# A scheduler's clock that counts stores with the loads, and a last weight matrix whose preparation yields between its steps

## The chip, the cores and the metric

The kernel runs on one core of one Trainium2 chip. The metric is the device time of one execution in microseconds. One execution was recorded by the hardware profiler; all durations below are from that record unless another source is named.

## The reference, cut to what matters

One layer of an encoder reads 2048 prompt frames and 64 frames of running streams. After a differential attention (branch A, result `oa`) and a retention (branch B, result `ob`), both of width 512, the layer ends like this:

```python
oa = (rmsnorm(oa, subln_g) * (1.0 - lam_init)).reshape(B, T, W_A) * jax.nn.silu(za)
ob = rmsnorm(ob).reshape(B, T, W_B) * jax.nn.silu(zb)
m = ga * (oa @ w_oa) + gb * (ob @ w_ob)     # w_oa, w_ob: 512 x 1024; ga, gb: sigmoid gates
return x + m @ w_out                        # w_out: 1024 x 1024
```

The two products with `w_oa` and `w_ob` are called the branch products here, and `w_out` is the last matrix. Everything is fp32.

## The kernel before, in words

**How order comes about.** The program is written by a planner that runs while the kernel is built. Work is cut into Python generators (tasks). `loop` takes the task with the lowest priority number that is not asleep, lets it emit its next instructions, and puts it to sleep until the time, or the condition, that it yields. The planner's clock is `self.pe`; it advances with each matmul emitted. Estimated ends on the other engines are kept in `self.act`, `self.dve`, `self.pool`, and the end of the loads in `self.dma`: `ld` adds a load's bytes at 230 or 300 bytes per ns to `self.dma`, and a load counts as landed `DMA_LAT` later. `st` gives a store its own time and leaves `self.dma` alone. A task that waits for a tile in memory sleeps until that estimate. What is emitted this way becomes a fixed order on PE, ACT, DVE and POOL, and each of them executes in that order, so an instruction whose data is late holds up all behind it. All DMAs are issued by one queue, SP.

**The high and low split.** Each fp32 operand of a matmul is split in two: ACT casts the high half (names in `h`), DVE or POOL subtracts it to get the low half (names in `l`). Each product takes three matmuls: high by high, high by low, low by high.

**The stage of the branch products** runs from about 1575 us to 1773 us. The columns are taken in 8 groups of 264 (256 prompt columns and 8 of the sample). For every group, `og_fin` brings in 4 tiles each of branch A and of branch B: DMA loads `z` and `on`, ACT takes the SiLU of `z`, POOL multiplies (`on`), ACT casts `ogh`, DVE subtracts `ogl`. Then `m_tile` computes 8 tiles of 128 output rows; a tile is 24 matmuls (lines 1722 to 1724), 12 into a bank with tag `mm` (branch A) and 12 into one with tag `s` (branch B); both tags have two banks. `m_fin` ends a tile: DVE multiplies each bank with its gate (`gt`, line 1742) and so frees the bank, POOL adds the two (line 1746), SP stores the sum into `mT` in HBM. The gates of a tile are loaded (`gaT`, `gbT`) and put through a tanh on ACT (line 1698). There are five pairs of gate tiles, so a pair is loaded again only when its store has landed. There is room for three half groups of `ogh`, `ogl` (tags `og` and `ob`): the half for branch B of the next group can be cast only when branch A of the last tile of the present group has been multiplied.

**The last matrix beside it.** `b_prep` works through `w_out` in four steps (c = 0 to 3). `b_raw` loads four 128x512 blocks (`wst`), of which DVE forms the sums and differences t1 to t4 of a seven-product scheme (line 1758), and `b_split` makes high and low halves: `bh`, `bl` of the plain blocks, `bht`, `blt` of the sums of c = 0, 1 (lines 1815, 1818), and, after the weights of the branch products are free, `wot` for those of c = 2, 3 (`b_late`). `b_prep` has priority 2, the branch products 8. In `out_prep`, which loads `z` and `on`, the condition `b_left < 13` lets the four loads of c = 0 go ahead of the second group.

**The last stage** (`y_group`, from about 1773 us) takes the groups again. `y_load` reads four blocks `a` of `mT` back per group, `y_prep` forms s1 and s2 on DVE and s3 and s4 on POOL (`a<-a`) and splits all of them (`ah` on ACT, `al` on DVE, line 1860); seven products P1 to P7 of 12 matmuls each follow (line 1934), in the order P1, P2, P6, P5, P7, P3, P4. `y_out` moves them: ACT copies `u`, POOL adds the loaded input `oxt` (line 1756), DVE adds the bank (line 1984: `u<-s` for P2, `u<-mm` for P7, `u<-at` for P3, `oxt<-mm` for P4). P4 of a group is followed on PE by P1 of the next.

Of the kernel before, what the change touches and what calls it, by code (L numbers as in the profile page):

```python
# [37 lines left out]
SLACK = 400.0  # L38
PACE = 700.0
DMA_LAT = 2600.0  # L40
QUANT = 6


# [16 lines left out]
class Hybrid:  # L60
# [72 lines left out]

    def ld(self, dst, src, nbytes=0):
        self.nc.sync.dma_start(dst, src)
        self.dma = max(self.dma, self.pe) + nbytes / (300.0 if self.opened else 230.0)
        return self.dma + DMA_LAT

    def st(self, dst, src, nbytes=0):
        self.nc.sync.dma_start(dst, src)  # L140
        return self.pe + nbytes / 150.0 + DMA_LAT

    def psum(self, tag):
        return self.pp.tile([128, 512], F32, tag=tag, name=tag, bufs=BUFS[tag])
# [1487 lines left out]
            yield self.pe  # L1632

    def out_prep(self):
        pa = self.z3p
        self.wo = [[([[self.sb(self.zq, [128, 512], "wa", "woq", F32R) for n in "hl"],
                      [pa.tile([128, 512], F32R, tag=f"wo{n}{br}{kt}", name=f"wo{n}{br}{kt}") for n in "hl"]], {})
                    for kt in range(4)] for br in range(2)]
        for br in range(2):
            yield from self.load_wo(br, 0)  # L1640
        for g in range(8):
            gsl = slice(GW * g, GW * g + GW)
            for br, (oT, zT) in enumerate(((self.oaT, self.zaT), (self.obT, self.zbT))):
                for kt in range(4):
                    yield from self.take("oz", 2)
                    on = self.sb(pa, [128, GW], "oz", "on")
                    z = self.sb(pa, [128, GW], "oz", "z")
                    self.ld(z, zT[kt][:, gsl], 1 << 17)
                    t = self.ld(on, oT[kt][:, gsl], 1 << 17)
                    og = []  # L1650
                    self.ogs.append(og)
                    self.spawn(self.og_fin(on, z, t, og, (2 * g + br) % 3 == 2), 1)
                    yield self.pe
            if g == 0:
                self.spawn(self.gates(), 0)
# [105 lines left out]
    def b_raw(self, c, pool, tag):  # L1761
        w = self.i["w_out"][0]
        raw = {}
        for k, r, n in (("11", c, 0), ("12", c, 512), ("22", c + 4, 512), ("21", c + 4, 0)):
            yield from self.take(tag)
            raw[k] = self.sb(pool, [128, 512], tag, "wst")
            t = self.ld(raw[k], w[128 * r:128 * r + 128, n:n + 512], 1 << 18)
            self.b_left -= 1
        yield t + 600
        return raw  # L1770

    def b_prep(self):
        late = []
        for c in range(4):
            raw = yield from self.b_raw(c, self.z4, "st")
            for k in ("t1", "t2"):
                yield from self.take("st")
                raw[k] = self.sb(self.z4, [128, 512], "st", "wst")
            t1 = self.add(False, ALU.subtract, raw["t1"], raw["12"], raw["11"], self.pe)
            for k in ("11", "21", "22"):  # L1780
                t = yield from self.b_split(k, c, raw[k], self.pe)
            t3 = self.add(False, ALU.subtract, raw["12"], raw["22"], raw["12"], t)
# [4 lines left out]
            yield t2  # L1787
            t4 = self.add(False, ALU.subtract, raw["21"], raw["21"], raw["t2"], t2)
            parts = [("t2", c, raw["t2"], t4), ("t1", c, raw["t1"], t1), ("t3", c, raw["12"], t3),
                     ("t4", c, raw["21"], t4)]  # L1790
            if c < 2:
                yield from self.b_fin(parts)
            else:
                late.append(parts)
        self.spawn(self.b_late([p for pair in zip(*late) for p in pair]), 1)
        self.spawn(self.y_prep(), 1)

    def b_fin(self, parts):
        for k, c, s, t in parts:
            t = yield from self.b_split(k, c, s, t)  # L1800
            self.give("st", t)

    def b_late(self, parts):
        yield lambda: self.q_end is not None
        yield self.q_end
        yield from self.b_fin(parts)
# [368 lines left out]
    def run(self):  # L2175
# [20 lines left out]
        self.b_left = 16  # L2196
        for k in ("ac", "u", "xt", "ob"):
            self.res[k].free = []
        self.q_end = self.smx = None
        self.y_at, self.yr = -1, []  # L2200
        self.yq = [{} for _ in range(8)]
        ET = mybir.EngineType
# [93 lines left out]
```

## Time and profile before

| what | value |
|---|---|
| median of 3 runs (lowest, highest) | 1945.87 us (1943.82, 1946.53) |
| the profiled execution: its own time, its span | 1945.82 us, 1944.0 us |
| PE busy, share of the span | 1927.5 us, 99% |
| DVE, ACT, POOL busy | 1166.6, 964.9, 490.1 us |
| moved by DMA, mean rate | 303.32 MB, 156 GB/s |
| granted TensorE clock, mean | 0.998 |

PE is busy nearly all the time, so time is lost where PE stands and where its clock is lowered; the other engines and the DMAs matter only where PE waits for them. "PE busy" takes in the modelled ends of the matmuls, which overlap. In a list of waits, the first name is who waits, the second for whom; the columns are the total in us, how often, and the longest. A row of a timeline gives the start, the duration, the engine, the line and the operation, `out<-in`, the count, and in brackets how long the engine had stood idle before and what ended that.

### The profile page before, as it was taken

To read this page: it belongs to the slowest core of one execution; us is meant where nothing else is said; L and a number is where in the kernel's file an instruction comes from. 1 tells how busy PE (TensorE), PEld (TensorE's weight loads), DVE (VectorE), ACT (ScalarE), POOL (GpSimd) and SP (SyncE) were. 2 spreads that over 40 slices of the span, in tenths; PEclk is the share of its full clock that TensorE was granted. 3 is DMA by queue.
4 is the path that set the end of the run, shared out by engine and by line. 5 is a ranking of instruction groups with operands and counts; after the bars stand their busy time and mean duration, and the time that the engine had idled before them with its cause. 6 is when DMAs were issued, how large, how long until landed. Compare 5 with 4: busy or idle time off the path is not lost.

```text
span 1944.0 us, 33842 instructions
## 1 busy us (share of the span) xinstructions
PE 1927.5 (99%) x11984; PEld 1731.2 (89%) x11984; DVE 1166.6 (60%) x2798; ACT 964.9 (50%) x2072; POOL 490.1 (25%) x429
## 2 busy tenths in 40 slices
PE   9999999999999999999999999999999999999999
PEld 8779999999988899999998888888888889998887
DVE  6753777646666336648856757845773376545643
ACT  7443766544434235535765646544563445653321
POOL 4310112112122121211121111112113356543422
PEclk9999999999999999999999999999999999999999
DMA  7747454335566655654344253363133678866651
GB/s 235 240 151 199 143 143 132 106 102 156 163 192 187 166 148 168 202 183 141 112 120 128 76 146 96 99 185 116 63 99 108 190 229 259 264 196 189 190 151 65
DMA packets 372074, 303.32 MB, mean 156 GB/s; under 512 B 77440, under 2 KB 334720, under 8 KB 371904
## 3 DMA queue, kind: packets, MB, share of 16 engines
q1 hardware_dynamic: 371904, 301.16, 52.6%
q8 instruction: 94, 1.54, 0.4%
q14 instruction: 76, 0.62, 0.1%
HBM read 195.87 MB, written 100.14 MB: 152 GB/s over the span
## 4 chain that ended last, share of the span: by engine, by line
PE 88%; DVE 5%; DMA 3%; POOL 1%; issue 1%; ACT 1%; SPq 1%; DVEq 0%; POOLq 0%; ACTq 0%
PE mm L554 51%; PE mm L1934 4%; PE s L1052 3%; PE s L1053 3%; PE at L1160 3%; PE at L1934 2%; PE pv L1139 2%; PE pv L1140 2%; PE pv L1138 2%; PE s L1934 1%; PE s L1723 1%; PE s L1724 1%; PE pv L1521 1%; PE mm L1723 1%; PE s L1722 1%
## 5 line engine op out<-in xcount | busy, mean ns | idle before, releaser
L514 POOL TENSOR_TENSOR wl<-ws,wh 128x512 fp32r<-128x512 f32 x191 | 261.4, 1380 | 896.2 <-ACT wh L504 544.9
L554 PE MATMUL mm<-xh,wh 128*128 128x512 f32 (+2 forms) x1280 | 460.7, 360 | 0.0
L554 PE MATMUL mm<-xh,wl 128*128 128x512 f32 (+2 forms) x1280 | 452.7, 354 | 0.0
L554 PE MATMUL mm<-xl,wh 128*128 128x512 f32 (+2 forms) x1280 | 451.9, 353 | 0.0
L554 PEld LDWEIGHTS mm<-xh,wl 128*128 128x128 f32 x1280 | 241.0, 188 | 31.7
L554 PEld LDWEIGHTS mm<-xh,wh 128*128 128x128 f32 x1280 | 241.4, 189 | 29.1 <-issue 0.2
L554 PEld LDWEIGHTS mm<-xl,wh 128*128 128x128 f32 x1280 | 241.6, 189 | 27.8
L554 PE MATMUL mm<-wh,xh 128*128 128x256 f32 (+1 forms) x768 | 236.7, 308 | 0.0
L554 PE MATMUL mm<-wh,xl 128*128 128x256 f32 (+1 forms) x768 | 231.3, 301 | 0.0
L554 PE MATMUL mm<-wl,xh 128*128 128x256 f32 (+1 forms) x768 | 231.0, 301 | 0.0
L1175 DVE TENSOR_TENSOR atl<-at,ath 128x512 fp32r<-128x512 f32 (+1 forms) x144 | 93.7, 659 | 136.2 <-ACT ath L1173 136.1
L504 ACT CAST wh<-ws 128x512 fp32r<-128x512 f32 x192 | 117.0, 617 | 112.6 <-PE mm L554 90.3
L1091 ACT ACTIVATE row<-row,a_mx 128x1024 f32<-128x1024 f32 (+7 forms) x160 | 153.7, 962 | 24.5 <-DVE a_mx L1071 24.3
L554 PEld LDWEIGHTS mm<-wh,xh 128*128 128x128 f32 x768 | 146.3, 190 | 7.1 <-issue 0.5
L554 PEld LDWEIGHTS mm<-wl,xh 128*128 128x128 f32 x768 | 146.4, 191 | 6.7 <-issue 0.5
L554 PEld LDWEIGHTS mm<-wh,xl 128*128 128x128 f32 x768 | 146.3, 190 | 5.5
L865 DVE TENSOR_TENSOR ev<-mm,rsb 128x512 f32<-128x512 f32 x140 | 83.0, 593 | 112.8 <-PE mm L554 112.4
L1173 ACT CAST ath<-at 128x512 fp32r<-128x512 f32 (+1 forms) x144 | 78.7, 563 | 141.5 <-PE at L1160 138.4
L1061 DVE CUSTOM_DVE_ANT_0 row<-s,dfar 128x512 f32<-128x512 f32 (+2 forms) x192 | 118.2, 630 | 46.4 <-PE s L1053 45.9
L1052 PE MATMUL s<-K,q 128*128 128x512 f32 (+3 forms) x320 | 118.4, 374 | 0.7 <-DVE a_acc L1061 0.7
L1053 PE MATMUL s<-K,q 128*128 128x512 f32 (+3 forms) x320 | 115.2, 362 | 0.0
L1110 ACT ACTIVATE row<-row,a_w 128x1024 f32<-128x1024 f32 (+4 forms) x96 | 85.1, 898 | 34.4 <-DVE a_w L1105 31.2
(342 smaller groups left out, 4193.5 us busy)
## 6 DMA issues: line engine op xcount, KB each, us to landing
ws<-in_w_in_dram SPq DMA_DIRECT2D x192, 256.0 KB, 3.1
q<-qT SPq DMA_DIRECT2D x128, 128.0 KB, 3.0
V<-vN SPq DMA_DIRECT2D x24, 512.0 KB, 5.4
K<-kT SPq DMA_DIRECT2D x48, 256.0 KB, 4.3
a<-mT SPq DMA_DIRECT2D x34, 256.0 KB, 4.1
gt<-gaT SPq DMA_DIRECT2D x64, 132.0 KB, 3.2
gt<-gbT SPq DMA_DIRECT2D x64, 132.0 KB, 3.1
mT<-gt SPq DMA_DIRECT2D x64, 132.0 KB, 3.0
```

What stands on the lines that cost most here:

```text
L504: self.nc.scalar.copy(h, st)
L514: self.nc.gpsimd.tensor_sub(l, st, h.bitcast(F32))
L554: nc.tensor.matmul(ps, p, q, start=c == 0 and i == 0, stop=c == KC - 1 and i == 2)
L865: nc.vector.tensor_mul(ev, ps, rsb)
L1052: nc.tensor.matmul(ps, q1s, kk, start=True, stop=False)
L1053: nc.tensor.matmul(ps, q2s, kk, start=False, stop=True)
L1061: nc.vector.tensor_tensor_reduce(out=units[k0 // 1024][:, k0 % 1024:k0 % 1024 + n], in0=ps, in1=tab, scale=-SLOPES[h], scalar=3.0e38, op0= ...
L1091: nc.scalar.activation(u, u, AF.Exp, bias=mx, scale=-1.0, accum_out=lp[:, k:k + 1])
L1110: nc.scalar.activation(u1, u1, AF.Identity, scale=w[:, 1:2])
L1173: nc.scalar.copy(ah[:, :w], at[:, :w])
L1175: nc.vector.tensor_sub(al[:, :w], at[:, :w], ah[:, :w].bitcast(F32))
L1934: nc.tensor.matmul(q[b], u, v, start=fresh and c == 0 and m == 0, stop=c == 3 and m == 2, skip_group_check=True)
```

## The change

Three things are changed, all in the planner; no arithmetic is added or taken away. From `out_prep` on (`packed`), loads count at 265 bytes per ns, and stores are counted on the same clock. The preparation of the last matrix yields for 1500 ns of the planner's clock between its loads and between its steps, and the condition `b_left` goes. `y_load`, which read `mT` back when all four `t4` were emitted, waits for three `t1`.

```diff
+RATE = 265.0
     def ld(self, dst, src, nbytes=0):
-        self.dma = max(self.dma, self.pe) + nbytes / (300.0 if self.opened else 230.0)
+        self.dma = max(self.dma, self.pe) + nbytes / (RATE if self.packed else 300.0 if self.opened else 230.0)
     def st(self, dst, src, nbytes=0):
-        return self.pe + nbytes / 150.0 + DMA_LAT
+        if self.packed:
+            self.dma = max(self.dma, self.pe) + nbytes / RATE
+        return max(self.packed * self.dma, self.pe + nbytes / 150.0) + DMA_LAT
     def out_prep(self):
+        self.packed = 1
...
-                yield lambda: self.b_left < 13
...     # b_raw, after each load
-            self.b_left -= 1
-        yield t + 600
+            yield self.pe + 1500
+        if t + 600 > self.pe:
+            yield t + 600
...     # b_prep, after t1, after each split, after t3 and t2; b_fin likewise for c < 2
+            yield self.pe + 1500
-            yield t3
+            yield max(t3, self.pe + 1500)
     def y_load(self):
-        yield lambda: len(self.wt["t4"]) == 4
+        yield lambda: len(self.wt["t1"]) > 2
```

On PE the two programs have the same rows in the same order, numbers of tiles and lines apart. On the other engines and on SP the order differs from the branch products on. (The lines of the changed file are 1 to 8 higher: 135 becomes 136, 1680 becomes 1683, 1818 becomes 1826.)

SP, in group 1's first tiles, where `z` and `on` of group 2's branch B are loaded. Before:

```order
L135 DMA z<-zbT 128x264
L135 DMA on<-obT 128x264
L135 DMA wst<-in_w_out_dram 128x512 x4
L135 DMA z<-zbT 128x264
L135 DMA on<-obT 128x264
L135 DMA gt<-gaT 128x264
L135 DMA gt<-gbT 128x264
```

And now, from the same pair of loads on:

```order
L136 DMA z<-zbT 128x264
L141 DMA mT<-gt 128x264
L136 DMA on<-obT 128x264
L136 DMA gt<-gaT 128x264
L136 DMA gt<-gbT 128x264
L136 DMA z<-zbT 128x264
L136 DMA gt<-gaT 128x264
L136 DMA on<-obT 128x264
L136 DMA gt<-gbT 128x264
```

The four loads of c = 1 left this place; they stand 33 to 40 issues later, each between gate loads and stores, and those of c = 2 and c = 3 moved by 38 to 67 and by 80 to 90 issues.

DVE, in group 1, ahead of the eight `ogl` for branch B of group 2 and branch A of group 3. Before:

```order
L1758 TENSOR_TENSOR wst<-wst 128x512
L1742 SCALAR_TENSOR_TENSOR gt<-gt,mm 128x264
L1742 SCALAR_TENSOR_TENSOR gt<-gt,s 128x264
L1758 TENSOR_TENSOR wst<-wst 128x512
L1742 SCALAR_TENSOR_TENSOR gt<-gt,mm 128x264
L1742 SCALAR_TENSOR_TENSOR gt<-gt,s 128x264
L1818 TENSOR_TENSOR blt_18302<-wst,bht_18301 128x512
L1818 TENSOR_TENSOR blt_18300<-wst,bht_18299 128x512
L1742 SCALAR_TENSOR_TENSOR gt<-gt,mm 128x264
L1742 SCALAR_TENSOR_TENSOR gt<-gt,s 128x264
L1818 TENSOR_TENSOR blt_18304<-wst,bht_18303 128x512
L1680 TENSOR_TENSOR ogl<-on,ogh 128x264 x8
```

And now:

```order
L1826 TENSOR_TENSOR blt_18326<-wst,bht_18325 128x512
L1745 SCALAR_TENSOR_TENSOR gt<-gt,mm 128x264
L1745 SCALAR_TENSOR_TENSOR gt<-gt,s 128x264
L1826 TENSOR_TENSOR blt_18328<-wst,bht_18327 128x512
L1745 SCALAR_TENSOR_TENSOR gt<-gt,mm 128x264
L1745 SCALAR_TENSOR_TENSOR gt<-gt,s 128x264
L1745 SCALAR_TENSOR_TENSOR gt<-gt,mm 128x264
L1745 SCALAR_TENSOR_TENSOR gt<-gt,s 128x264
L1683 TENSOR_TENSOR ogl<-on,ogh 128x264 x8
```

Before, this is work on c = 1, whose blocks were loaded in the place shown above; now it is work on c = 0, at most one instruction between two tiles, and two whole tiles stand between the last of it and the `ogl`.

DVE at the passage to the last stage, from the last tile's `gt` on: s1, s2 of group 0, its low halves, the additions after P2, P7, P3 and P4, and the low halves of group 1. Before:

```order
L1742 SCALAR_TENSOR_TENSOR gt<-gt,s 128x264
L1758 TENSOR_TENSOR a<-a 128x512 x2
L1860 TENSOR_TENSOR al<-a,ah 128x512
L1984 TENSOR_TENSOR u<-s,u 128x512
L1860 TENSOR_TENSOR al<-a,ah 128x512 x4
L1984 TENSOR_TENSOR u<-mm,u 128x512
L1984 TENSOR_TENSOR u<-at,u 128x512
L1860 TENSOR_TENSOR al<-a,ah 128x512 x2
L1758 TENSOR_TENSOR a<-a 128x512
L1984 TENSOR_TENSOR oxt<-mm,oxt 128x512
```

And now:

```order
L1745 SCALAR_TENSOR_TENSOR gt<-gt,s 128x264
L1761 TENSOR_TENSOR a<-a 128x512
L1868 TENSOR_TENSOR al<-a,ah 128x512 x5
L1992 TENSOR_TENSOR u<-s,u 128x512
L1992 TENSOR_TENSOR u<-mm,u 128x512
L1992 TENSOR_TENSOR u<-at,u 128x512
L1992 TENSOR_TENSOR oxt<-mm,oxt 128x512
L1868 TENSOR_TENSOR al<-a,ah 128x512 x2
L1761 TENSOR_TENSOR a<-a 128x512 x2
```

All five low halves of group 0 now stand ahead of the addition after P2, and the first two of group 1 behind the addition after P4.

POOL at the same place: the last tiles' sums (`gt`), the additions of the input (`u<-u,oxt`), and s4 and s3 of groups 0 and 1 (`a<-a`). Before:

```order
L1746 TENSOR_TENSOR gt<-gt 128x264 x15
L1756 TENSOR_TENSOR u<-u,oxt 128x512
L1756 TENSOR_TENSOR a<-a 128x512 x2
L1756 TENSOR_TENSOR u<-u,oxt 128x512 x2
L1756 TENSOR_TENSOR a<-a 128x512 x2
```

And now:

```order
L1749 TENSOR_TENSOR gt<-gt 128x264 x14
L1759 TENSOR_TENSOR a<-a 128x512 x2
L1759 TENSOR_TENSOR u<-u,oxt 128x512 x3
L1759 TENSOR_TENSOR a<-a 128x512 x2
L1759 TENSOR_TENSOR u<-u,oxt 128x512 x3
```

The first addition of the input, which stood ahead of s4 and s3 of group 0, stands behind them.

More of the change, by code (lines that the diff above doesn't have):

```diff
@@ L1779, in b_prep @@
             t1 = self.add(False, ALU.subtract, raw["t1"], raw["12"], raw["11"], self.pe)
+            yield self.pe + 1500
             for k in ("11", "21", "22"):
                 t = yield from self.b_split(k, c, raw[k], self.pe)
+                yield self.pe + 1500
             t3 = self.add(False, ALU.subtract, raw["12"], raw["22"], raw["12"], t)
             self.give("st", t3)
-            yield t3
+            yield max(t3, self.pe + 1500)
             t2 = self.add(False, ALU.add, raw["t2"], raw["12"], raw["11"], t3)
             self.give("st", t2)
-            yield t2
+            yield max(t2, self.pe + 1500)
             t4 = self.add(False, ALU.subtract, raw["21"], raw["21"], raw["t2"], t2)
@@ L1801, in b_fin @@
             self.give("st", t)
+            if c < 2:
+                yield self.pe + 1500
     def b_late(self, parts):
@@ L2195, in run @@
         self.wt = {k: [] for k in BLOCKS}
-        self.b_left = 16
         for k in ("ac", "u", "xt", "ob"):
@@ L2199, in run @@
         self.q_end = self.smx = None
+        self.packed = 0
         self.y_at, self.yr = -1, []
```

## The prediction

> **What bounds the kernel now.** I read the page first: PE is busy for 99% of the span, so only what stops PE or slows its clock counts. The orders differ only from the branch products on, so the question is what PE loses after about 1536 us. The list of PE's waits from 1500 us to the end answers it (who waits, for whom, total us, times, longest):
>
> ```profile
> span 1944.0 us, 33842 instructions
> PE s L1723 <- DVE ogl L1680: 3.0, 6, 1.7
> PE s L1722 <- ACT ogh L1677: 1.1, 1, 1.1
> PE at L1934 <- DVE al L1860: 1.1, 1, 1.1
> PE mm L1722 <- DVE gt L1742: 0.8, 1, 0.8
> PE mm L1934 <- ACT u L1962: 0.7, 1, 0.7
> ```
>
> That is 6.7 us in all, and all of it in places that the change rewrites. The busy times by stretches show where, and what else is lost (columns: length, PE, PEld, DVE, ACT, POOL busy, then the granted clock, the DMA share, GB/s):
>
> ```profile
> 1584.00:1596.00 12.00, 11.21 (x90) 10.83 (x89) 12.00 (x19) 8.71 (x22) 9.51 (x11) 1.00 0.71 213
> 1608.00:1620.00 12.00, 12.00 (x101) 12.00 (x100) 8.70 (x15) 7.13 (x16) 8.96 (x10) 1.00 0.93 289
> 1620.00:1632.00 12.00, 9.22 (x59) 8.81 (x59) 8.56 (x17) 9.53 (x25) 4.72 (x6) 0.81 0.80 241
> 1632.00:1644.00 12.00, 12.00 (x93) 12.00 (x92) 5.62 (x11) 4.89 (x11) 7.88 (x9) 0.91 0.80 252
> 1776.00:1788.00 12.00, 10.19 (x43) 7.74 (x42) 4.33 (x6) 4.26 (x8) 5.89 (x5) 1.00 0.80 266
> ```
>
> The third stretch holds the big loss: PE stands 2.8 us, and behind that the clock is lowered. 12 us at 0.81 and 12 at 0.91 are 2.3 + 1.1 = 3.4 us of lost clock. The fourth row shows it as the lower count of matmuls, 93 where an undisturbed stretch has 101. So all that there is to gain is 6.7 + 3.4 = 10.1 us, 0.5% of the time. DVE is busy for all of the first stretch, and the DMA engines at 0.93 in the second: these two are what makes PE wait.
>
> **The big wait (1624 to 1628 us).** PE reaches branch B of group 2. Its casts stand on ACT, its low halves on DVE, and both queues are held by the last matrix. The queue rows, SP first, then ACT, then DVE:
>
> ```profile
> 1603.22 2.55 SPq L135 DMA_DIRECT2D wst<-in_w_out_dram  x4
> 1618.63 0.38 SPq L135 DMA_DIRECT2D z<-zaT  x1
> 1620.13 1.65 SPq L135 DMA_DIRECT2D gt<-gbT  x1
> ```
>
> ```profile
> 1622.90 0.42 ACT L1664 ACTIVATE z<-z 128x264 f32<-128x264 f32 x1 [1.32 <-DMA z<-zaT]
> 1623.23 1.12 ACT L1815 CAST bht<-wst 128x512 fp32r<-128x512 f32 x2
> 1624.26 0.92 ACT L1698 ACTIVATE gt<-gt,bg 128x264 f32<-128x264 f32 x2
> 1625.08 0.60 ACT L1815 CAST bht<-wst 128x512 fp32r<-128x512 f32 x1
> 1625.59 2.60 ACT L1677 CAST ogh<-on 128x264 fp32r<-128x264 f32 x8
> ```
>
> ```profile
> 1623.87 2.05 DVE L1818 TENSOR_TENSOR blt<-wst,bht 128x512 fp32r<-128x512 f32 x2 [2.75 <-ACT bht L1815]
> 1626.52 0.68 DVE L1818 TENSOR_TENSOR blt<-wst,bht 128x512 fp32r<-128x512 f32 x1
> 1627.12 3.25 DVE L1680 TENSOR_TENSOR ogl<-on,ogh 128x264 fp32r<-128x264 f32 x6
> ```
>
> ACT stands 1.3 us for a late `z`, then casts three `bht` and only then `ogh`; DVE stands 2.75 us for the `bht`, then makes three `blt` and only then `ogl`. The change moves all of this: c = 1's loads are gone from SP's queue there (2.55 us of issue, and 1.05 MB, 3.6 us at 289 GB/s), the three `bht` ahead of the casts (1.7 us on ACT), and the `blt` ahead of the `ogl` (2.7 us on DVE). What remains ahead of the casts are the tanh of tiles 15 and 16 and `z` of group 3. From both sides: the `blt` alone are as long as PE's idle time, so all 2.8 us can go, and the clock's 3.4 with them; or the last gate pair stays late by itself (it waited 1.65 us at SP) and nothing goes. I take the upper end, since SP comes to that pair at least 2.55 us earlier, less the 0.3 us that the other group starts also lose: **-5.9**.
>
> On the clock the row comes first: 3.4 us were lost behind a gap of 2.8 us. The Trainium skill (TensorE: Matmul & The Clock Gate, Part 1) says that an idle window of about 3.4 us halves the clock until a window of that length was busy again. By that the loss would be half of 3.4, 1.7 us, and the sum 1.7 smaller. The trace shows twice that and after a shorter gap; I go by the trace.
>
> **The first wait (1590 us).** DVE runs c = 0's work as soon as its loads land, and the bank of tile 3 is freed late:
>
> ```profile
> 1586.73 1.24 DVE L1818 TENSOR_TENSOR bl<-wst,bh 128x512 fp32r<-128x512 f32 x1
> 1587.89 1.24 DVE L1758 TENSOR_TENSOR wst<-wst 128x512 f32<-128x512 f32 x1
> 1589.05 0.98 DVE L1680 TENSOR_TENSOR ogl<-on,ogh 128x264 fp32r<-128x264 f32 x1
> 1590.43 0.39 PE L1722 MATMUL mm<-ogh,woh 128*128 128x264 f32 x1 [0.79 <-DVE gt L1742]
> ```
>
> Now the gates of tiles 0 to 3 stand ahead of all this work, then one instruction of it per tile. 1.24 us fits beside a tile of 24 matmuls (24 x 12 / 101 = 2.9 us). **-0.8**; bounds 0 and -0.8.
>
> **The other group starts.** The five shorter waits for `ogl` are 3.0 - 1.7 = 1.3 us. For groups 3 to 6 the casts now stand behind the tanh of one tile less, and three or four `ogl` come before the last tile's gate in groups 3 to 5 instead of one or two. In group 6 a `wst` falls between two `ogl` (0.9 us), though. I take half: **-0.6**, between -1.3 and +0.9.
>
> **The passage to the last stage.** Two waits, 1.1 + 0.7 us. These are their rows, from PE, POOL, DVE and ACT:
>
> ```profile
> 1782.98 0.50 PE L1934 MATMUL at<-bht,al 128*128 128x512 f32 x1 [1.07 <-DVE al L1860]
> 1786.30 0.50 PE L1934 MATMUL mm<-bht,ah 128*128 128x512 f32 x1 [0.74 <-ACT u L1962]
> 1779.85 1.29 POOL L1756 TENSOR_TENSOR u<-u,oxt 128x512 f32<-128x512 f32 x1 [4.97 <-DMA oxt<-in_x_prompt_dram]
> 1781.10 2.96 POOL L1756 TENSOR_TENSOR a<-a 128x512 f32<-128x512 f32 x2
> 1781.18 0.69 DVE L1984 TENSOR_TENSOR u<-s,u 128x512 f32<-128x512 f32 x1 [2.49 <-POOL u L1756]
> 1784.10 1.66 ACT L1853 CAST ah<-a 128x512 fp32r<-128x512 f32 x3 [5.67 <-POOL a L1756]
> 1792.77 1.28 DVE L1860 TENSOR_TENSOR al<-a,ah 128x512 fp32r<-128x512 f32 x2
> 1794.96 0.69 DVE L1984 TENSOR_TENSOR oxt<-mm,oxt 128x512 f32<-128x512 f32 x1 [0.29 <-PE mm L1934]
> ```
>
> POOL stands 5 us for an input load, with s4 and s3 behind it; DVE stands 2.5 us for that same addition, with the low half for P5 behind it. Both now stand the other way round, and s4 and s3 can run 5 us earlier: **-1.8**. But the last row shows the price. The addition after P4 waits for PE's last product of the group, and group 1's first low halves, which stood ahead of it, now stand behind. PE's third matmul of P1 needs one: 0.29 us until DVE wakes, 0.69 for the addition, 0.64 for a low half (1.28 / 2), less the 0.4 us that the first two matmuls cover, **+1.2**. Bounds: 0.7 if DVE wakes at once and +2.0 if the low half takes twice as long beside POOL.
>
> SP also asks for group 1's `a` ahead of the ten `oxt` now. The third waits for POOL, so the additions on POOL may come later by the 3 us that s4 and s3 take; the addition that P4 needs has more time than that (P7 and P3, 24 matmuls), so I cost it at nothing. If it were late, P4 would wait up to that.
>
> **A new place.** Between the gates of tile 7 and of tile 8, DVE now has three `ogl`, a `wst` and three `ogl` (before: one, a `blt`, two):
>
> ```profile
> L1680 DVE TENSOR_TENSOR ogl<-on,ogh 128x264 fp32r<-128x264 f32 x56 | 30.7, 597 | 9.5 <-ACT ogh L1677 7.1 <-PE s L1724 2.4
> L1742 DVE SCALAR_TENSOR_TENSOR gt<-gt,s 128x264 f32<-128x264 f32 x62 | 26.3, 425 | 35.1 <-PE s L1724 26.8 <-ACT z L1664 3.1 <-ACT bh L1815 1.1
> L1758 DVE TENSOR_TENSOR wst<-wst 128x512 f32<-128x512 f32 x15 | 13.4, 895 | 0.0
> ```
>
> 6 x 0.60 + 0.90 + 2 x 0.43 = 5.3 us, against two tiles, 5.7 us, until PE wants the bank. With the long durations seen above (0.98 and 1.24) it is 8.0 us. **+0.4**, between 0 and 2.3.
>
> The planner's 265 bytes per ns itself costs nothing on the chip; its price is the places it gives. The Trainium skill (DMA: Bandwidth & Descriptors, Specifications) puts a core's share of HBM at about 358 GB/s. The trace has 289 at a DMA share of 0.93, above 265 too. A planner that counted with the page's figure would hold the last `a` of group 1 for landed earlier; if that kept the low halves ahead of the addition, the sum would be 1.2 better.
>
> **Sum.** -5.9 - 0.8 - 0.6 - 1.8 + 1.2 + 0.4 = -7.5 us. The profiled execution took 1945.8 us, 0.05 from the median of the runs, so the forecast is 1938.3 us.
>
> **The rivals.**
>
> 1. *The big wait stays.* The last gate pair is loaded only when the store of tile 11 has landed, and its tanh still stands ahead of the casts. Should ACT still come to them late, the 5.9 stay: 1945.8 - 0.8 - 0.6 - 1.8 + 1.2 + 0.4 = 1944.2. For it speaks the row with 1.65 us at SP; against it that DVE then held up tile 11's gate itself, by work that is now elsewhere.
>
> 2. *Slower: the wait is moved, not removed.* The blocks c = 2 and c = 3 now fall into groups 4 to 6, which had no such work. If there too a `bh` or `wst` on late data stands ahead of a group's `ogh` and `ogl`, each such start costs what it cost at 1624 us, 2.8 + 3.4 = 6.2. One brings 1944.5, no change; two bring 1950.7, slower. It decides when PE's gap is long enough for the clock to fall, nearly 3 us; the wait of 1.07 us at 1783 did not lower it (1.00 in that stretch). Against it: in most of these places the gates stand between, one instruction per tile.
>
> 3. *The change does little that counts.* The bytes are the same, and with DMA engines at 0.8 to 0.9 every load stays late wherever it stands: 1945 or so. Against it: PE had stretches without a wait at 0.93.
>
> **How the numbers follow.** 0.2% is 3.9 us, about what a measurement here can tell from no change. Forecast 0.57, between 1935 (nearly all of the 10.1 gained) and 1942; the big wait stays 0.20; moved waits 0.19, of which slower 0.14; little that counts 0.04. So faster 0.57, the same 0.29, slower 0.14. The range of 1935 to 1949.5 leaves the slower cases out above and a few parts in 100 below.
>
> **What would show it.** Right: no stretch between 1584 and 1770 us with a clock under 1.00; the list of PE's waits without the 1.1 us for `ogh` and the 1.7 for `ogl`, nothing over 0.3 us for `gt`; P5 and P7 of group 0 without a wait; a new wait of about 1 us of `mm` at the first low half of group 1, for DVE `al`. Wrong: another stretch with a clock near 0.8, a wait for `gt` at tile 10 above 1 us, or P4 of group 0 waiting for the additions behind the `oxt` loads.

## The result: slower by 0.23%

The changed kernel takes 1949.92 us (median of 12 runs, 1946.82 to 1951.49), the kernel before 1945.45 us beside it (12 runs). The ratio is 1.0023, 95% interval 1.0014 to 1.0032: 4.5 us slower, where 7.5 us less was forecast. Two executions that took far longer, one of the kernel before (3162 us) and one of e12 (6130 us), are left out of all ratios below.

The list of PE's waits from 1500 us on, changed kernel (who waits, for whom, total us, times, longest):

```profile
PE mm L1725 <- DVE gt L1745: 4.8, 7, 1.9
PE mm L1725 <- ACT z L1667: 3.0, 1, 3.0
PE mm L1942 <- DVE al L1868: 0.9, 1, 0.9
PE s L1726 <- DVE ogl L1683: 0.3, 1, 0.3
```

Every wait of the list before is gone or nearly so, and the sum is 9.0 us instead of 6.7. The new ones have another form: PE wants a bank (`mm`), which the last gate of an earlier tile has not left. The windows show where it costs clock (length, PE, PEld, DVE, ACT, POOL busy, granted clock, DMA share, GB/s):

```profile
1572.00:1584.00 12.00, 10.10 (x67) 9.15 (x65) 2.25 (x6) 2.55 (x7) 2.60 (x4) 1.00 0.64 188
1584.00:1596.00 12.00, 10.90 (x68) 10.93 (x69) 5.91 (x13) 4.98 (x13) 9.00 (x12) 0.72 0.86 272
1620.00:1632.00 12.00, 11.74 (x96) 11.43 (x95) 6.81 (x14) 8.46 (x22) 5.75 (x7) 1.00 0.87 257
1716.00:1728.00 12.00, 9.55 (x64) 9.13 (x62) 6.31 (x11) 7.92 (x18) 6.98 (x8) 0.86 0.87 257
```

The stretch at 1620 us, which had the clock of 0.81, is clean. But 12 us at 0.72 (3.4 us) now stand in group 0 and 12 at 0.86 (1.7 us) in group 5. From the starts of the matmuls in the two traces, the length of each group of the branch products (first matmul to first matmul of the next, us), and of the last stage (first matmul to the start of its last one):

| | start | 0 | 1 | 2 | 3 | 4 | 5 | 6 | 7 | last stage |
|---|---|---|---|---|---|---|---|---|---|---|
| before | 1574.90 | 24.64 | 23.81 | 29.49 | 23.94 | 24.80 | 23.83 | 24.23 | 23.39 | 166.99 |
| changed | 1576.11 | 29.23 | 23.36 | 24.13 | 24.04 | 25.78 | 28.07 | 24.03 | 23.61 | 165.93 |

An undisturbed group takes 23.4. Group 2 gained 5.4; group 0 lost 4.6, groups 4 and 5 lost 5.2; the last stage gained 1.1. The 1.2 us at the start are not the change: PE is as late as that from 612 us on, and the orders of the other queues part only at 1534 us. In later traces the start lies between 1574.3 and 1578.0.

**The stop in group 0**, timeline of the changed kernel, SP, ACT, DVE, PE:

```profile
1578.79 0.38 SPq L141 DMA_DIRECT2D gbT<-ev  x1
1582.74 0.81 SPq L136 DMA_DIRECT2D wst<-in_w_out_dram  x2
1582.70 0.41 ACT L1680 CAST ogh<-on 128x264 fp32r<-128x264 f32 x1 [7.67 <-DMA gbT<-ev]
1583.15 0.43 DVE L1683 TENSOR_TENSOR ogl<-on,ogh 128x264 fp32r<-128x264 f32 x1 [6.15 <-ACT ogh L1680]
1583.77 0.84 DVE L1683 TENSOR_TENSOR ogl<-on,ogh 128x264 fp32r<-128x264 f32 x1 [0.19 <-ACT ogh L1680]
1584.53 0.42 DVE L1745 SCALAR_TENSOR_TENSOR gt<-gt,mm 128x264 f32<-128x264 f32 x1
1585.10 0.56 PE L1725 MATMUL mm<-ogh,woq 128*128 128x264 f32 x1 [3.00 <-ACT z L1667]
```

The first row is the last store of the stage before (`gbT<-ev`). When it has landed, at 1582.7, two things go on at once: SP's first load of `w_out` and ACT's first cast for group 1. Both write to memory (the pool `z4`, with the tags `st` and `ob`) that lies where `ev` lay. DVE has two low halves of group 1 ahead of tile 0's gate, so DVE stands 6.15 us, the gate comes at 1584.53, and PE, which wants that bank for tile 2, stands 3.0 us. (The profile names ACT's `z`, which ended at the same moment; the bank is freed by the gate, which ended at 1584.95.) The order on DVE there:

```
L868 TENSOR_TENSOR ev<-mm,rsb 128x512
L1683 TENSOR_TENSOR ogl<-on,ogh 128x264 x2
L1745 SCALAR_TENSOR_TENSOR gt<-gt,mm 128x264
L1745 SCALAR_TENSOR_TENSOR gt<-gt,s 128x264
```

Before, the gates of tiles 0 and 1 followed `ev` directly: the condition `b_left` held back group 1's loads, and with them its low halves. The rows of before, DVE and SP, and one line of SP's list of waits from 1500 us on:

```profile
1575.10 0.69 DVE L865 TENSOR_TENSOR ev<-mm,rsb 128x512 f32<-128x512 f32 x1 [4.76 <-PE mm L554]
1576.57 0.43 DVE L1742 SCALAR_TENSOR_TENSOR gt<-gt,mm 128x264 f32<-128x264 f32 x1 [0.78 <-PE mm L1724]
1578.13 1.76 SPq L135 DMA_DIRECT2D wst<-in_w_out_dram  x4
SPq L135 <- DMA gbT<-ev: 1.8, 1, 1.8
```

The wait for the store was there too: SP's first load of `w_out` stood 1.8 us for it. It cost PE nothing there, since the gates of tiles 0 and 1 stood ahead of all that waited.

**The stop in group 5**, the same view, ACT, DVE, PE:

```profile
1720.73 0.43 ACT L1667 ACTIVATE z<-z 128x264 f32<-128x264 f32 x1 [1.57 <-DMA z<-zaT]
1721.06 0.60 ACT L1823 CAST bh<-wst 128x512 fp32r<-128x512 f32 x1
1721.70 1.12 DVE L1826 TENSOR_TENSOR bl<-wst,bh 128x512 fp32r<-128x512 f32 x1 [2.45 <-ACT bh L1823]
1722.74 0.42 DVE L1745 SCALAR_TENSOR_TENSOR gt<-gt,mm 128x264 f32<-128x264 f32 x1
1723.21 0.39 PE L1725 MATMUL mm<-ogh,woh 128*128 128x264 f32 x1 [1.87 <-DVE gt L1745]
```

A late `z` on ACT, behind it the cast of a block of the last matrix, behind that its low half on DVE, behind that a gate, behind that PE. The waits at 1665, 1689 and 1696 us show the same chain; at 1718 the gate's own tanh stands behind a late `z`, and at 1748 the pieces are an `ah` and `al` of the last stage, behind a load of `a`.

**The passage**, DVE and PE:

```profile
1784.33 1.90 DVE L1868 TENSOR_TENSOR al<-a,ah 128x512 fp32r<-128x512 f32 x3 [0.23 <-ACT ah L1861]
1789.07 0.69 DVE L1992 TENSOR_TENSOR u<-s,u 128x512 f32<-128x512 f32 x1 [2.84 <-POOL u L1759]
1798.04 0.69 DVE L1992 TENSOR_TENSOR oxt<-mm,oxt 128x512 f32<-128x512 f32 x1 [2.08 <-PE mm L1942]
1798.65 1.28 DVE L1868 TENSOR_TENSOR al<-a,ah 128x512 fp32r<-128x512 f32 x2
1799.38 0.50 PE L1942 MATMUL mm<-bh,al 128*128 128x512 f32 x1 [0.92 <-DVE al L1868]
```

The addition after P2 still waits for POOL, but with all low halves done, so P5 and P7 wait for nothing; the one wait left is the new one that was forecast, 0.92 us.

### The profile page after: what moved, and what is told of

Same layout as the page of the kernel before. It is cut to its first block, busy times and chain, and to the rows that moved or that the text cites. A ratio compares the mean times of both kernels' runs of the same rounds, so it can differ in the third digit from the quotient of the medians.

```text
span 1948.3 us, 33875 instructions
## 1 busy us (share of the span) xinstructions
PE 1929.0 (99%) x11984; PEld 1733.0 (89%) x11984; DVE 1158.1 (59%) x2798; ACT 966.0 (50%) x2072; POOL 487.6 (25%) x429
## 4 chain that ended last, share of the span: by engine, by line
PE 88%; DVE 4%; DMA 3%; ACT 2%; issue 1%; SPq 1%; POOL 1%; DVEq 0%; ACTq 0%; POOLq 0%
PE mm L557 50%; PE mm L1942 5%; PE s L1055 3%; PE s L1056 3%; PE at L1163 3%; PE at L1942 2%; PE pv L1142 2%; PE pv L1143 2%; PE pv L1141 2%; DMA mT<-gt 1%; PE s L1942 1%; PE mm L1725 1%; PE s L1726 1%; PE mm L1726 1%; PE mm L1727 1%
## 5 line engine op out<-in xcount | busy, mean ns | idle before, releaser
L557 PEld LDWEIGHTS mm<-xl,wh 128*128 128x128 f32 x1280 | 241.6, 189 | 27.8
L1094 ACT ACTIVATE row<-row,a_mx 128x1024 f32<-128x1024 f32 (+7 forms) x160 | 153.7, 962 | 24.6 <-DVE a_mx L1074 24.5
```

The source lines that it names most:

```text
L557: nc.tensor.matmul(ps, p, q, start=c == 0 and i == 0, stop=c == KC - 1 and i == 2)
L1094: nc.scalar.activation(u, u, AF.Exp, bias=mx, scale=-1.0, accum_out=lp[:, k:k + 1])
```

## The experiments

Fifteen kernels, each timed in 5 rounds beside the kernel before, whose median was 1946.4, 1945.0, 1945.8 and 1944.6 us in the four sessions (e1 to e4, e5 to e8, e9 to e12, e13 to e15). So the ratios are compared. "Waits" is the sum of PE's waits from 1500 us on; "half" counts the stretches of 3.41 us at half clock in the records of the trace (6.83 are two); "branch" and "last" are the lengths of the two stages. Waits and the rest are of one profiled execution. Each ratio is known to about 0.0009, so a difference of two of them to about 0.0013.

| kernel | ratio to before (95%) | waits | half | branch | last |
|---|---|---|---|---|---|
| before | 1 | 6.7 | 2 | 198.1 | 167.0 |
| changed | 1.0023 (1.0014 to 1.0032) | 9.0 | 3 | 202.2 | 165.9 |
| e1 old condition | 0.9998 (0.9990 to 1.0007) | 5.8 | 2 | 197.5 | 165.9 |
| e2 `ob` free later | 0.9998 (0.9990 to 1.0007) | 8.7 | 1 | 197.7 | 168.5 |
| e3 new clock alone | 1.0020 (1.0012 to 1.0029) | 9.7 | 2 | 196.3 | 171.2 |
| e4 old clock | 0.9999 (0.9991 to 1.0008) | 9.4 | 2 | 197.6 | 170.6 |
| e5 e2 + slack | 1.0001 (0.9992 to 1.0009) | 6.8 | 0 | 195.9 | 167.2 |
| e6 e1 + slack | 0.9987 (0.9978 to 0.9996) | 4.7 | 0 | 193.3 | 165.8 |
| e7 e1 + 4000 ns | 0.9979 (0.9970 to 0.9987) | 4.0 | 2 | 194.4 | 166.0 |
| e8 old `y_load` | 1.0023 (1.0014 to 1.0031) | 9.9 | 2 | 195.7 | 171.5 |
| e9 before + 4000 ns | 0.9991 (0.9982 to 1.0000) | 4.4 | 1 | 195.5 | 164.6 |
| e10 changed + 4000 ns | 0.9997 (0.9988 to 1.0006) | 6.2 | 0 | 194.9 | 166.0 |
| e11 e2 + 4000 ns, late start | 1.0018 (1.0009 to 1.0027) | 10.4 | 2 | 202.8 | 166.6 |
| e12 e6 + 4000 ns | 1.0024 (1.0015 to 1.0033) | 9.6 | 3 | 192.9 | 174.0 |
| e13 e8, one addition later | 1.0009 (1.0000 to 1.0018) | 7.6 | 1 | 197.1 | 166.5 |
| e14 e12, one addition later | 0.9996 (0.9988 to 1.0005) | 7.0 | 0 | 192.3 | 169.3 |
| e15 e7, one sum later | 0.9994 (0.9985 to 1.0003) | 3.8 | 1 | 193.9 | 166.0 |

Waits plus 1.7 us for each half stretch is roughly what PE lost: 10.1 us before, 14.1 changed. (Where PE stands inside such a stretch the two overlap; in e12 PE stood for nearly all of one of the three, so 1.7 us are counted twice.) For some kernels the difference to before goes with the ratio (times 1945 us): changed +4.0 against +4.5, e11 +3.7 against +3.5, e3 +3.0 against +3.9, e7 -2.7 against -4.1. In eight of the sixteen it misses by 2 to 3.5 us (most in e5, -3.3 against +0.2). The trace is one run and need not be a typical one: the profiled runs of e2 and e4 (1949.98 and 1949.29 us) lie about 3 us above their medians, those of e9, e10 and e15 2 us and more below.

The mean granted clock is on record for every run. Averaged over a kernel's runs it is 0.9997 and 0.9999 for e5 and e10, whose traces have no fall, but 0.9993 and 0.9990 for e6 and e14, whose traces have none either; e8 and e12 have the lowest, 0.9979 and 0.9974. The changed kernel has 0.9984, the kernel before 0.9984 to 0.9989 in the four sessions. So over all runs the clock makes about 1 us of the 4.5 at most, and most of it is PE standing, as far as three places of the clock tell.

### What stops group 0: e1, e2, e4

e1 puts the old condition back into the changed kernel; e2 tells the planner when that memory comes free; e4 leaves `packed` at 0.

```diff
     # e1: b_raw, after each load; out_prep, after a group
+            self.b_left -= 1
+                yield lambda: self.b_left < 13
     # e2: w_stream
-        self.give("ob", self.pe, BUFS["ob"])
+        self.give("ob", max(self.res["ev"].free), BUFS["ob"])
     # e4: out_prep
-        self.packed = 1
+        self.packed = 0
```

> The changed kernel with the old condition kept: group 1's z and on loads wait until c = 0's four loads have been issued. In the order this puts the gates of tiles 0 to 3 ahead of the first low half of group 1. Theory A (the door): what cost most is that two ogl of group 1, which lie in memory that only comes free when the last store of gbT has landed, stand ahead of tile 0's gate on DVE; so the stop of 3.3 us near 1582 goes, and the 6.8 us at half clock behind it: 1949.9 - 3.0 - 3.4 = 1943.5. Theory B (the late store): the last store of gbT is late because SP's order and the planner's clock changed, whatever stands behind it; then a stop of 2 us or more near 1582 stays, about 1950. Under both, the waits of PE for gates behind a low half in groups 3 to 6 (4.8 us in all, one of 1.9) stay.

> The changed kernel in which the planner is told when that memory comes free: the eight places of tag ob are given at the planned landing of the last evacuation store instead of at once. Nothing else differs. In the order tile 0's gate then stands ahead of all four ogl of group 1, but the gate of tile 1 behind them. Theory A: the stop near 1582 goes if the store lands before tile 2 is to start, at worst it moves one tile later and is shorter: 1943.5 to 1947. Theory B: as with the changed kernel, about 1950.

> The changed kernel with the old clock (230 or 300 bytes per ns, stores apart): the yields of the last matrix's work, the removed condition and the earlier reading back of mT stay. In the order four ogl of group 1, not two, stand ahead of tile 0's gate. Theory A: the stop near 1582 is there and at least as long (3.3 us or more, then two windows of half clock), about 1950 or above. Theory B: the new clock is what makes the store late, so the stop goes and the time is 1943 to 1946.

e1: the stop is gone, group 0 takes 23.2 us, and the ratio falls by 0.0025 (4.9 us; 6.4 were expected). e2: the stop moved one tile later and shrank to a gap of 1.3 us between matmuls, without a loss of clock; ratio 0.9998 too. For e1 and e2 theory A holds, except that in e1 the waits for gates, which were to stay, are gone (its list has 3.0 us for `ogh`, 1.9 for `ogl` and 0.9 for `al`). e4 goes against what A said: four low halves stand ahead of the gate there, and group 0 takes 23.4 us. SP, ACT and DVE of e4:

```profile
1576.20 0.37 SPq L141 DMA_DIRECT2D gbT<-ev  x1
1578.53 1.36 ACT L1680 CAST ogh<-on 128x264 fp32r<-128x264 f32 x4 [5.28 <-DMA gbT<-ev]
1580.36 0.42 DVE L1745 SCALAR_TENSOR_TENSOR gt<-gt,mm 128x264 f32<-128x264 f32 x1
```

The last store is issued 2.6 us earlier than in the changed kernel and has landed at 1578.5, 4.2 us earlier (0.8 of it because the stage starts earlier); the gate comes at 1580.4, still in time for tile 2. So each theory had half: the stop takes both, low halves in the freed memory ahead of the gate (no condition any more) and a store that SP issues late, behind five loads, and that lands 3.9 us after its issue began (2.3 in e4). Either alone costs nothing (e1's store landed at 1580.6, with nothing behind it that a gate needed).

### The waits for gates in groups 3 to 6: e3, e5, e6

e3 is the kernel before with the first two pieces of the diff alone (`RATE`, `ld`, `st`, `packed`). e5 and e6 put a gate between a cast and its low half:

```diff
     # b_split, not for the late blocks
-        yield t
+        yield t if k[0] == "t" and c > 1 else max(t, self.pe + 3000)
         self.nc.vector.tensor_sub(l, s, h.bitcast(F32))
```

> The kernel before with the new clock alone (265 bytes per ns, stores counted); the last matrix's work is bunched as before and the old condition stands. Theory A: no stop near 1582, since gates 0 and 1 stand first. Theory C (the low halves of the last matrix hold up gates wherever they stand singly between gates behind casts that wait for late z): bunched as it is here, the waits for gates are fewer; the sum of PE's waits from 1500 us on is then below the changed kernel's 9.0 and nearer to before's 6.7, the time 1940 to 1946. Against C: PE waits for gates as long as in the changed kernel, 1946 to 1950.

> The kernel of e2 in which the low half of a block of the last matrix is emitted 3000 ns of the planner's clock after its cast instead of at once, so that a tile's gate stands between them on DVE. Theory C (PE's waits for gates in groups 3 to 6 come from low halves that stand ahead of the gate and wait for a cast, which stands on ACT behind a z still being loaded): e2's 5.6 us of waits for gates fall to 1.5 or less, and with nothing put in their place the ratio to before goes from 0.9998 to 0.998 (some 4 us). Theory D (the loads are late wherever the work stands): the waits go over to ogh and ogl at the groups' starts, the sum of PE's waits stays between 7 and 10 us and the ratio within 0.999 to 1.001.

> The kernel of e1 with the same 3000 ns between cast and low half. e1 had no waits for gates, but 3.0 us for ogh and 1.9 for ogl. Theory C: little changes in the waits for gates (none to remove); the same ratio as e1, 0.9998, within 0.001. Theory D: the sum of PE's waits, 5.8 us in e1, is again between 5 and 8, whatever it is that waits. A ratio under 0.998 would be against both.

e3 has no stop near 1582, and its groups 4 to 7 take 23.4 to 23.7 us: the block work is over by then, as before. The kernels with the new yields, and with neither the slack nor the later landing, all lose 2 us or more in one of these groups (changed 28.1 in group 5, e1 27.2 and 27.8 in 5 and 6, e2 25.9 and 25.4, e4 29.4 in group 4, e8 26.8 and e13 28.7 in 5; in e1 the stops are waits for `ogh` and `ogl`). So the yields brought stops into these groups. In e3 the waits for gates are 3.6 us, fewer than 4.8, but all waits are 9.7, not below 9.0; its ratio, 1.0020, is made in the last stage, which takes 171.2 us (below). The lists of waits of e2 and of e5 show C's chain cut:

```profile
PE mm L1725 <- DVE gt L1745: 5.6, 6, 1.3
PE mm L1942 <- ACT ah L1861: 1.9, 1, 1.9
PE s L1726 <- DVE ogl L1683: 1.2, 4, 0.4
```

```profile
PE s L1726 <- DVE ogl L1683: 3.9, 9, 0.9
PE mm L1725 <- DVE gt L1745: 1.2, 1, 1.2
PE mm L1942 <- DVE al L1868: 0.9, 1, 0.9
PE mm L1942 <- ACT ah L1861: 0.8, 1, 0.8
```

The waits for gates fall from 5.6 to 1.2, as C said, but 2.7 us come back as waits for `ogl`, as D said (the sum, 6.8, is just under D's 7 to 10), and the ratio does not move. So what C's chain costs in the medians is not shown: where it was cut, other waits took its place. With the old condition (e6) it goes to 0.9987, a little outside what C gave; the sum of the waits is 4.7, under D's 5 to 8, and none of them lowers the clock.

### Data that the planner believes to be there: e7, e9, e10, e11, e12

```diff
     def ld(self, dst, src, nbytes=0):
-        return self.dma + DMA_LAT
+        return self.dma + (4000.0 if self.packed else DMA_LAT)
     # e11 also: b_prep, ahead of its loop
+        yield self.pe + 24000
```

> The kernel of e1 in which the planner holds a load for landed 4000 ns after its bytes are counted, not 2600, from the branch products on; so z, the gates' tanh and the blocks' casts are emitted 1.4 us later than before, and casts whose data is there stand ahead of them. Theory D (what stops PE is work on late data at the head of an in-order queue, and the planner believes that data to be there): the waits for ogh and ogl at the starts of groups fall from 4.9 us to 2 or less, no window of half clock is left in the branch products, and the ratio is 0.997 (5 us). Against D: the same waits as in e1, ratio 0.9998, or new waits because everything comes later, ratio above 1.001.

> The kernel before, with one number changed: from the branch products on a load counts as landed 4000 ns after its bytes, not 2600. Rates, stores, the last matrix's bunched work, the condition and the reading back of mT stay as before. Theory D (in-order queues stand at work whose data the planner believes to be there): the big stop in group 2 (group 2 takes 29.5 us in the kernel before, an undisturbed group 23.4) shrinks by half or more, and the ratio is 0.998 or below. Theory E (the later landing helps only together with the last matrix's work spread out and the early reading back): group 2 stays above 27 us or the passage to the last stage costs more; ratio 0.999 to 1.002.

> The changed kernel with the same 4000 ns and nothing else. In the order tile 0's gate then stands ahead of the first low half of group 1, and one gate between each of the others. Theory A and D: group 0 falls from 29.2 us to 24.5 or less, the waits for gates in groups 3 to 6 (2.9 us) by half or more; ratio 0.998 (against 1.0023 for the changed kernel). Against them: the ratio stays at 1.000 or above, since the old condition that e7 had is what mattered.

> e2 with the 4000 ns, and the last matrix's work starts 24 us of the planner's clock later, so that nothing of it stands in group 0 and little in group 1. Theory D: e7's one stop (2.6 us and two windows of half clock in group 1, at two sums of the last matrix between low halves on DVE) goes, no group takes more than 24.5 us; ratio 0.996 (8 us). Against it: the work comes too late for the last stage (the passage longer than 20.5 us for its first seven products) or stops PE in groups 2 to 6 instead; ratio 0.998 to 1.000.

> e7 with e6's 3000 ns between cast and low half as well. Theory D: the two measures act at the same waits, so they don't add up: ratio 0.997 to 0.998, as e7. If they are separate (late z at the casts; a block's cast at its own low half), the gains add to 0.9966 (0.9979 less 0.0013).

In three pairs the 1.4 us later landing made the kernel faster: e1 to e7 by 0.0019, before to e9 by 0.0009 (the interval ends at 1), changed to e10 by 0.0026. e7 is the best of all: 0.21% under the kernel before, and by the two ratios 0.44% under the changed one. Two thirds of what D gave it came (0.9979 from e1's 0.9998, not 0.997): the waits for `ogl` are 3.1 us, where 2 or less were forecast, one of them 2.6 with two stretches of half clock. Its waits:

```profile
PE s L1728 <- DVE ogl L1685: 3.1, 3, 2.6
PE mm L1945 <- DVE al L1871: 0.9, 1, 0.9
```

And those of e9, which differs from the kernel before by this one number; group 2 fell from 29.5 to 24.1 us, and no wait is left in the last stage, but group 0 rose to 27.4:

```profile
PE mm L1724 <- DVE gt L1744: 2.0, 1, 2.0
PE s L1725 <- DVE ogl L1682: 1.4, 3, 0.9
PE s L1724 <- ACT ogh L1679: 1.0, 1, 1.0
```

In e10 group 0 takes 23.4 us; the waits for gates did not fall by half (4.6 us in all, 4.8 in the changed kernel, where the expectation had 2.9), but none lowers the clock. So D's direction holds three times, with half to two thirds of its size, and the big stop of group 2 goes without any change to the block work. But e12 (1.0024, against 0.9987 for e6) shows that it is no lever that always works, and neither side had forecast that. e11 (1.0018, against 0.9998 for e2) changes two things; the later landing alone was not tried on e2. In e11 groups 1, 4 and 5 take 27.4, 26.0 and 29.3 us, with 8.1 us of waits for gates: the block work that starts later stands at other gates. In e12 the branch products are short, 192.9 us, and the last stage loses 8 us.

### The passage to the last stage: e8, e13, e14

e8 puts `len(self.wt["t4"]) == 4` back into `y_load`. e13 and e14 are e8 and e12 with one instruction moved:

```diff
     # y_out, ahead of the addition on DVE
+        if (g, p) == (0, "P2"):
+            t = max(t, self.pe + 6000)
```

> The changed kernel with y_load's old condition (mT is read back when all four t4 are there). In the order the first low halves of group 1 stand ahead of the addition after P4 again, and the addition after P2 ahead of five low halves of group 0. The prediction's terms: the new wait of 0.9 us of PE for the first low half of group 1 goes, and P5 and P7 of group 0 wait again, 1 to 1.8 us in all; so the last stage is 0 to 1 us longer than the changed kernel's 165.9. The stop near 1582 and the waits for gates do not depend on it (theory A): they stay, and the ratio is 1.002 to 1.003. If the ratio is 1.000, the order that the early reading back gives, not the first group, is what cost.

> The kernel of e8 with one instruction moved: on DVE the addition after P2 of group 0, which waits for an input load and an addition on POOL, stands behind four low halves of group 0 instead of ahead of all five; nothing else differs in any queue. Theory F (the passage to the last stage is set by how many low halves stand behind that addition: none ahead cost 3.9 us and two windows of half clock in e8, one ahead 1.8 in the kernel before, three or more nothing): the last stage falls from 171.5 to 164.6 to 166 us and the ratio from 1.0023 to 0.999. Against F: the low halves are late by themselves (their casts or s1 to s4), the stop of 3.8 us stays and the ratio is 1.002.

> The kernel of e12 with the same instruction moved in the same way and nothing else. Theory F: e12's branch products (192.9 us, the shortest of all) stay, its last stage falls from 174.0 to 166 or less, ratio 0.9985 or less (from 1.0024); 0.997 if the wait for ah of 2.1 us goes too. Against F: 1.001 or more.

e8, from POOL, DVE and PE:

```profile
1777.12 1.26 POOL L1759 TENSOR_TENSOR u<-u,oxt 128x512 f32<-128x512 f32 x1 [5.01 <-DMA oxt<-in_x_prompt_dram]
1778.42 0.69 DVE L1992 TENSOR_TENSOR u<-s,u 128x512 f32<-128x512 f32 x1 [5.75 <-POOL u L1759]
1779.03 4.85 DVE L1868 TENSOR_TENSOR al<-a,ah 128x512 fp32r<-128x512 f32 x5
1780.21 0.80 PE L1942 MATMUL mm<-bht,al 128*128 128x512 f32 x1 [3.84 <-DVE al L1868]
```

The addition waits for POOL, which waits for an input load, with all five low halves behind it; PE stands 3.84 us at P6 and the clock falls. So in the profiled runs the last stage is 5.6 us longer without the early reading back (171.5 against 165.9), not 0 to 1 as I expected. The medians do not show this: the ratio is the same, 1.0023. Up to 1769 us e8 has the order of the changed kernel in every queue, and in the profiled run its branch products were shorter (195.7 us against 202.2; its stop in group 0 cost no clock, group 0 took 25.7 us). But that is one run against one, and why the medians agree stays open. e13 has this order too, and there group 0 took 26.4 us. So the 29.2 us of the changed kernel's trace are the longest of three runs of one order; that the stop costs something in the medians is shown by e1 and e2.

e13, from DVE and PE:

```profile
1777.67 1.29 DVE L1868 TENSOR_TENSOR al<-a,ah 128x512 fp32r<-128x512 f32 x2 [2.56 <-ACT ah L1861]
1785.18 0.69 DVE L1994 TENSOR_TENSOR u<-s,u 128x512 f32<-128x512 f32 x1
1785.51 0.50 PE L1942 MATMUL mm<-bht,ah 128*128 128x512 f32 x1 [1.64 <-ACT u L1970]
```

One instruction, moved behind four low halves, takes 5.0 us from the last stage (171.5 to 166.5), and 4.7 in e14 (174.0 to 169.3); theory F holds for the stop, though the last stages stay above its 166. The full gain does not come: P7 now waits 1.6 to 1.7 us for `u`, and in e14 the 2.2 us for `ah` stay. The ratios fall by 0.0014 and 0.0028, where 0.0033 and 0.0039 were forecast; the first is hardly clear of noise. Over the traces: with none of group 0's last five low halves ahead of that addition PE waits 3.8 to 4.0 us for `al` (e3, e8, e12), with one 1.1 (before), with three or more at most 0.3 (in e2 and e4 it waits 1.9 and 3.9 us for `ah` there).

### Group 1 of e7: e15

```diff
     # b_prep, ahead of t2
-            yield max(t3, self.pe + 1500)
+            yield max(t3, self.pe + (4500 if c == 0 else 1500))
```

> The kernel of e7 with the sum t2 of c = 0 emitted 4500 ns instead of 1500 ns behind t3, so that the two sums no longer stand together between low halves of group 1's branch B; what follows shifts with it. Theory D: e7's one stop (group 1, 29.0 us) goes, and if no other order suffers the ratio falls from 0.9979 to 0.995 (5.6 us less). Against it: the stop stays (the cast ogh was late too, 1.6 us behind POOL), or the shift puts a block's cast in front of another group's casts: 0.997 to 0.999.

The stop shrank from 2.6 to 1.4 us and group 1 from 29.0 to 27.3, with one stretch of half clock instead of two. But the ratio is 0.9994, above e7's 0.9979 and above what either side gave. The stop was not the two sums alone, as the order has one of them still between low halves of group 1, and the profiled run (1941.29 us) does not tell e15's median (1943.8); why its ratio is above e7's stays open.

## Why the prediction was wrong, point by point

**The big wait, -5.9: right.** Group 2 fell from 29.5 to 24.1 us, -5.4; the waits for `ogh` and `ogl` that made it are gone, and so is the clock loss there. The rival that it stays was wrong.

**The first wait, -0.8: the step that failed.** "Now the gates of tiles 0 to 3 stand ahead of all this work": that is true of the last matrix's work, but not of everything. Two low halves of group 1 stood ahead of tile 0's gate. I costed the removed condition `b_left` at nothing and did not ask what it had held back, nor what the memory of `ob` waits for. In the kernel before ACT shows nothing of it, since it stood there for a load; but SP's list of waits had the row, 1.8 us for `gbT<-ev`. Group 0 went from 24.6 to 29.2 us in the profiled runs: +4.6 instead of -0.8. In the medians e1, which takes this stop away and has others of its own, is 4.9 us faster, give or take 2.5.

**The other group starts and the new place, -0.6 and +0.4: sized right, and another place was missed.** The waits for `ogl` fell to 0.3 us, and the place at tile 10 cost nothing (group 1 takes 23.4). But the work taken out of group 2 went to groups 3 to 6, and there I counted its busy time only ("1.24 us fits beside a tile"). A low half that waits for its cast, behind a `z` still being loaded, holds the gate for that wait too: 2.45 us in the rows above. Groups 4 and 5 lost 5.2 us in the profiled run; how much of it is left in the medians is not shown (e5). What the second rival took as the argument against it, that gates stand between the pieces, is the mechanism: each piece between two gates is a place where a gate can be late.

**The passage, -1.8 + 1.2: right in kind.** Both old waits went, the new one is 0.92 us (1.2), the last stage is 1.1 us shorter (0.6). That without the early reading back the last stage would have been 5.6 us longer (e8's profiled run) was not seen: the order that it prevents appears in neither of the two kernels.

**The sum.** -7.5 against -5.4 + 4.6 + 5.2 - 1.1 - 0.3 (the other groups) + 1.2 (the start) = +4.2 in the profiled runs (1950.08 - 1945.82 = 4.26) and 4.5 in the medians. The rival "the wait is moved, not removed" had the price (1950.7, two places with loss of clock) and the general cause, but neither the places nor the waiting instruction: it looked at groups 4 to 6 alone, and one of the two places is group 0. That its price comes within 1 us of the result is luck, and I gave it too small a chance. The rival "little that counts" was wrong: single groups moved by up to 5.4 us.

**The clock.** The prediction took a gap of nearly 3 us as the point at which it falls. That was wrong as well; see the last section.

## What to carry to other kernels

When work is moved between the instructions of an in-order queue, count for each piece how long it may wait for its data, not only how long it is busy, and look at what stands behind it: here the instruction that frees a bank. When a condition is removed, look for everything that it held back, and for memory that is reused: a tile's first write can wait for a store of the stage before. And a planner that counts loads as landed too early puts late work at the heads of queues: one number (4000 ns for 2600) took the big stop out of the kernel before. At this size each new order brings stops of its own, so that only the chip tells which is best.

## What the runs showed of the hardware

**When the clock falls.** The changed kernel's stop in group 0 and that of e13, windows of 1 us (length, PE busy, clock, DMA share, GB/s). Changed:

```profile
1582.00:1583.00 1.00, 0.10 (x1) 1.00 0.01 3
1583.00:1584.00 1.00, 0.00 (x0) 1.00 0.30 39
1584.00:1585.00 1.00, 0.00 (x0) 0.56 0.87 268
1585.00:1586.00 1.00, 0.90 (x4) 0.50 0.96 313
```

And e13:

```profile
1582.00:1583.00 1.00, 0.00 (x0) 1.00 0.00 0
1583.00:1584.00 1.00, 0.00 (x0) 1.00 0.85 279
1584.00:1585.00 1.00, 0.56 (x4) 1.00 0.99 357
1585.00:1586.00 1.00, 1.00 (x11) 1.00 0.94 291
```

Stops of 3.00 and 2.79 us, and only one of them lowers the clock. In every trace the stretches of half clock are 3.41 us long or multiples of it and lie on a grid that is fixed within a trace. I laid that grid over all 17 traces, from the branch products on, and added up PE's idle time in each of its windows (starts of matmuls less their regular distance, 0.12 us at 264 columns, 0.23 at 512). All 17 falls follow a window with at least 1.95 us idle; the fullest windows that no fall followed have 1.95, 1.92 and 1.83. (The count is good to some 0.05 us, so at 1.95 falls and no falls meet.) In e13 the grid cuts the stop into 1.4 and 1.6 us. At half clock the same grid decides the return: after windows with up to 0.4 or 0.5 us of idle time the clock was full in the next one, after 0.8 or more it was not. By this a stop alone of under about 1.95 us costs its own length, and one between that and 3.9 us costs nothing more, 1.7 or 3.4 us more, as it falls on the grid. This can be one reason why runs of one kernel differ by some us: the mean clock of the changed kernel's 12 runs lies between 0.997 and 1.000.

The Trainium skill (TensorE: Matmul & The Clock Gate, Part 1) has the free-running window of 3413 ns, and the traces agree. The table in that part of the Trainium skill gives at least one idle window, about 3.4 us, for the lower clock; that the traces do not bear out, since 57% of one was enough.
